# A hybrid attention block: the gate projections as seven half-size products for each pair of column blocks

## The chip, the cores and the metric

The kernel runs on one core of one Trainium2 chip. The metric is the device time of one execution in microseconds (us); three runs of the kernel before gave a median of 1430.39 us (1430.27 to 1430.98). The profile is of one execution.

## What is computed

One encoder block on 1024 tokens of width 1024, with 16 meta tokens put in front and dropped again at the end, all in float32:

```python
h = concat([meta, x])
n = rms_norm(h, norm_mix)
qa, ka, va, qb, kb, vb, ga, gb = split(n @ w_in)     # 512, 512, 512, 512, 128, 128, 1024, 1024 columns
y_a = differential_attention(qa, ka, va, ...)        # branch A: 4 heads, all keys, two softmaxes subtracted
y_b = windowed_gqa(qb, kb, vb, sink)                 # branch B: 8 heads, window of 128, sinks
m = sigmoid(ga) * (y_a @ w_ba) + sigmoid(gb) * (y_b @ w_bb)
h = h + m @ w_o
h = h + swiglu(rms_norm(h, norm_ffn), w_gate, w_up, w_down)
out = rms_norm(h, norm_final)[16:]
```

The change concerns `ga` and `gb`: 2048 columns of `n @ w_in`, for the 1024 real tokens.

## The kernel before, in words

**Products.** The kernel keeps float32 accuracy with three matmuls of rounded operands. An operand is split (`split`, L114 to L117) into a high part, a copy that ScalarE (ACT) rounds, and a low part, the difference, made by GpSimd (POOL) or VectorE (DVE); a product is high x high + high x low + low x high. A group of matmuls gathers in one PSUM bank of 128 x 512 and is then evicted.

**The normalized input** stands in SBUF from the start of branch B to the end of branch A, transposed, as `hT_hi` and `hT_lo` (L173, L174): 128 partitions x 8 chunks of the width x 1088 tokens, the real ones at 0 to 1023, the meta tokens behind.

**Stages and their order.** (1) Norm and transposes of `x`, with the `kb` and `qb` projections between them, up to about 40 us. Behind them stands work on tables of distances (L558 to L600: an integer ramp from POOL; then on DVE conversion, negation and maximum for two halves, `far`, `tbx`, `lam_p`, `nsink`), and DVE's low half of the last `kb` eviction (L251). The `vb` projection follows (`project_v`, L604). (2) Branch B, from about 63 us to 293: units of `attend_b` between the other projections (`project_qa`, `project_kva`, `units_b`, L608 to L664). Queries, keys and values of branch A go to DRAM (`qa_d`, `ka_d`, `va_d`), B's results to `yb_d`. (3) Branch A with the gates, 293 to 622 us. (4) The merge, whose first products are `ppa` (`branch_mm`, L676): eight splits of `yb` (L929 to L939), four sigmoids at a time on loaded gates (`gated`, L987), a DVE multiplication (L1003). Then the output projection and the feed-forward part, which the change leaves alone.

**Weights.** `order` (L200 to L206) lists the column blocks of 128 in the order of use, and `ensure(n)` (L209) loads and splits them until n are ready. A block is 1024 x 128, loaded in one transfer of 512 KB into one of two raw buffers (`preload`, L186); ACT makes the high part whole, 128 x 1024, and POOL the low part (L116).

**Gates before.** `gate_steps` (L682) is a generator of 256 steps of three matmuls of 512 columns: 16 blocks x 2 halves of the tokens x 8 chunks. At the end of each half ACT copies the bank to `gate_stage` and SP stores it to `g_d`, from which the merge reads it.

**What sets the order in branch A.** PE's order is written out by hand (`tc.manual_schedule`, L827). A unit is one head and one tile of 128 queries; 32 units and one more run through a string of slots: `s` scores, `g` one gate step (`fill(1)`), `t` transposes, `n` the value products of earlier units. `SLOTS` (L41) has five `g`, `SLOTS_LAST` (L42), used for the last of the four heads, four. Ahead of head 0 stand `G_FIRST` = 30 gate steps, ahead of each other head `G_HEAD` = 10; `HOLD` = 36 steps are kept back for after the units (L805, L868 to L874). At the start of a head `load_a` (L705) issues the loads of its queries, keys and values. In a unit DVE finds the row minima out of PSUM (L741), combines the two softmaxes (L752, two SBUF operands of 128 x 1040), and makes the low part of the transposed weights (L768, out of PSUM); POOL scales one softmax (L749). The other engines' queues are ordered by the build's scheduler; SP's queue issues nearly all transfers in its order.

Of the kernel before, what the change touches and what calls it, by code (L numbers as in the profile page):

```python
# [9 lines left out]
F32 = mybir.dt.float32  # L10
F32R = mybir.dt.float32r
# [3 lines left out]
ALU = mybir.AluOpType  # L15
# [4 lines left out]
P = 128  # L20
# [53 lines left out]
def encoder_block(ctx: ExitStack, tc: tile.TileContext, x, meta, norm_mix, w_in, lq1, lk1, lq2, lk2,  # L74
# [7 lines left out]
    def f32(ap):  # L82
        return ap.bitcast(F32)
# [13 lines left out]
    def bank(p, tag, name, bufs):  # L97
        return p.tile([P, 512], F32, tag=tag, name=name, bufs=bufs)
# [2 lines left out]
    ka_d = [dram.tile([2, P, L], F32, name=f"ka_d{h}") for h in range(AH)]  # L101
    va_d = [dram.tile([P, 2, 9, P], F32, name=f"va_d{h}") for h in range(AH)]
    g_d = [dram.tile([P, S], F32, name=f"g_d{i}") for i in range(16)]
    ya_d = [dram.tile([P, S], F32, name=f"ya_d{h}") for h in range(4)]
    yb_d = [dram.tile([P, S], F32, name=f"yb_d{h}") for h in range(4)]

# [7 lines left out]
    def split(hi, lo, src, lo_eng):  # L114
        high = nc.scalar.activation(hi, src, AF.Copy)  # L115
        lo_eng.tensor_tensor(lo, src, f32(hi), ALU.subtract)  # L116
        return high  # L117
# [83 lines left out]
    for h in range(AH):  # L201
# [77 lines left out]
    def flush_v():  # L279
        for g in turning_v:  # L280
            for _ in g:
                pass
# [31 lines left out]
    def vb_evac(pt, k0, nb, kp):  # L314
        for g in range(BG):
            src = pt[:, :, 64 * g:64 * g + 64]
            hi = vb[g][:kp, k0:k0 + nb, 0:64]
            lo = vb[g][:kp, k0:k0 + nb, 64:128]
            nc.scalar.activation(hi, src, AF.Copy)
            nc.vector.tensor_tensor(lo, src, f32(hi), ALU.subtract)  # L320

    def new_qb(g):
        return bpool.tile([P, 4, S], F32R, tag="qb", name=f"qb{g}", bufs=1)
# [337 lines left out]
    for h in (2, 3):  # L661
        all_of(project_qa(h))
        project_kva(h)
    flush_v()  # L664
    close_bpool()
    close_psum1()

# [11 lines left out]
                nc.tensor.matmul(ps, w[:, a, j, :], src(j, b, tk),  # L679
                                 start=(j == 0 and n == 0), stop=(j == 3 and n == 2))  # L680

    def gate_steps():  # L682
        for i in range(16):
            def g_evac(ps, at, n, i=i):
                st = gstage.tile([P, 512], F32, tag="g", name="gate_stage", bufs=G_BUFS)
                nc.scalar.copy(st, ps)
                nc.sync.dma_start(g_d[i][:, at:at + n], st)

            ensure(1)
            col = (C_GB if i < 8 else C_GA) + (i % 8) * P  # L690
            for _ in project_steps(col, Q_CHUNKS, f"g{i}", g_evac):
                yield
            ensure(W_BUFS - 1)
# [5 lines left out]
    psum1 = psum2  # L699

    s0s = [apool.tile([P, 9 * P], F32, name=f"as0_{i}") for i in range(2)]
    for i in range(2):
# [897 lines left out]
```

## Time and profile before

| | |
|---|---|
| median of three runs | 1430.39 us |
| span of the profiled execution | 1427.5 us |
| outside the span, by these two | 2.9 us |
| matmul and transpose records of PE | 7279 |
| stage 1, norm and first projections | 0 to 63 us |
| branch B | 63 to 293.4 us |
| branch A with the gates | 293.4 to 621.6 us |
| gate matmuls | 768 of 512 columns |

The profile is of one execution: engines' busy time and its share of the span, the chain of work that ended last followed back from the end, groups of instructions by line, and DMA issues with the median time to landing. PE is the tensor engine's matmuls, PEld its weight loads, which overlap them, SP the queue that issues transfers. In a group's row, "x" is the count, then busy time in us and the mean of one in ns, then the idle time of the engine ahead of them and what ended it. In a timeline row the first two numbers are start and duration in us, and brackets hold the idle time ahead and its releaser. Line numbers are those of the kernel before.

### The profile page before, as it was taken

The page shows a single profiled execution, that of the slowest core. Times are in us where ns is not written, and L with a number is a line of the kernel's source. Part 1 is how long each engine was busy: PE and PEld are TensorE (multiplying, and loading weights), DVE is VectorE, ACT ScalarE, POOL GpSimd, SP SyncE. Part 2 cuts the span into 40 slices and gives each one's busy share as a digit, 9 for nine tenths or more (in the row PEclk, how much of TensorE's full clock was granted, in tenths as well). Part 3 has the DMA queues.
Part 4 walks back from the last instruction along what each step waited for, and adds up shares of the span by engine and source line. Part 5 has one row for each costly group of instructions (what it writes and reads, how often), then busy time and mean ns, then how long its engine had stood idle before and what let it go on. Part 6 is the DMA issues. An engine that isn't in the chain of part 4 may idle for free.

```text
span 1427.5 us, 20915 instructions
## 1 busy us (share of the span) xinstructions
PE 1418.5 (99%) x7279; PEld 1222.2 (86%) x7279; DVE 907.8 (64%) x1808; ACT 673.0 (47%) x1276; POOL 463.7 (32%) x462
## 2 busy tenths in 40 slices
PE   9999999999999999999999999999999999999998
PEld 8998999989898999888888888888888888888886
DVE  6555565528686868446978966555544553787566
ACT  6354555425454546455346654333333333444454
POOL 4143233322232222212503044454444442000442
PEclk9999999999999999999999999999999999999999
DMA  8443443381524252087432724423332232954443
GB/s 240 95 124 104 99 115 106 84 257 48 149 75 157 68 156 68 34 307 242 143 123 82 207 83 145 152 99 104 110 104 96 97 108 99 357 188 141 125 126 148
DMA packets 159018, 191.55 MB, mean 134 GB/s; under 512 B 16104, under 2 KB 103600, under 8 KB 158912
## 3 DMA queue, kind: packets, MB, share of 16 engines
q1 hardware_dynamic: 156992, 187.38, 41.4%
q10 hardware_dynamic: 1920, 2.83, 0.6%
q8 instruction: 58, 0.95, 0.3%
q14 instruction: 48, 0.39, 0.1%
HBM read 129.67 MB, written 53.94 MB: 129 GB/s over the span
## 4 chain that ended last, share of the span: by engine, by line
PE 96%; DMA 1%; DVE 1%; issue 0%; ACT 0%; POOL 0%; SPq 0%; DVEq 0%
PE pg L1363 29%; PE pd L1467 15%; PE pp_g L227 12%; PE ppa L679 5%; PE aps L735 4%; PE po L1266 4%; PE apy L777 3%; PE pp_ka L227 3%; PE pp_va L227 3%; PE pp_qb L227 3%; PE pp_qa L227 3%; PE apt L764 2%; PE bps L358 2%; PE po L1274 2%; PE bpy L398 1%; PE bpt L393 1%
## 5 line engine op out<-in xcount | busy, mean ns | idle before, releaser
L1363 PE MATMUL pg<-t,wop 128*128 128x512 f32 x1056 | 242.4, 389 | 0.0
L1363 PEld LDWEIGHTS pg<-t,wop 128*128 128x128 f32 x1056 | 198.3, 188 | 41.1
L1467 PE MATMUL pd<-ob,oa 128*128 128x512 f32 x924 | 209.6, 389 | 0.0
L1467 PEld LDWEIGHTS pd<-ob,oa 128*128 128x128 f32 x924 | 173.5, 188 | 36.0
L116 POOL TENSOR_TENSOR wop<-wf,wop 128x512 fp32r<-128x512 f32 x114 | 150.5, 1320 | 164.7 <-ACT wop L115 154.7
L1363 PE MATMUL pg<-b,wop 128*128 128x512 f32 x792 | 183.3, 389 | 0.0
L1363 PEld LDWEIGHTS pg<-b,wop 128*128 128x128 f32 x792 | 148.5, 188 | 30.7
L116 POOL TENSOR_TENSOR wl_c<-w_c,wh_c 128x1024 fp32r<-128x1024 f32 x32 | 77.4, 2419 | 137.4 <-ACT wh_c L115 115.7
L115 ACT ACTIVATE wop<-wf 128x512 fp32r<-128x512 f32 x128 | 80.8, 632 | 71.7 <-PE pg L1363 50.5
L746 ACT ACTIVATE as<-as,amn 128x1040 f32<-128x1040 f32 x64 | 74.5, 1165 | 73.8 <-DVE amn L741 73.7
L227 PE MATMUL pp_g<-hT_hi,wh_c 128*128 128x512 f32 x256 | 100.9, 394 | 0.0
L227 PE MATMUL pp_g<-hT_lo,wh_c 128*128 128x512 f32 x256 | 100.4, 392 | 0.0
L227 PE MATMUL pp_g<-hT_hi,wl_c 128*128 128x512 f32 x256 | 100.3, 392 | 0.0
L115 ACT ACTIVATE oa<-ra 128x512 fp32r<-128x512 f32 x77 | 48.7, 632 | 108.5 <-PE pd L1467 50.4
L735 PE MATMUL aps<-ak,aq 128*128 128x352 f32 (+1 forms) x384 | 93.0, 327 | 0.3 <-DMA ak<-ka_d 0.3
L116 POOL TENSOR_TENSOR oa<-ra,oa 128x512 fp32r<-128x512 f32 x27 | 34.9, 1294 | 168.6 <-ACT oa L115 167.2
L1140 DVE TENSOR_TENSOR s<-wf,wf 128x512 f32<-128x512 f32 x22 | 18.2, 827 | 110.4 <-DMA wf<-in_w_ff_up_dram 70.2
L735 PEld LDWEIGHTS aps<-ak,aq 128*128 128x128 f32 x384 | 69.7, 188 | 14.4 <-DMA ak<-ka_d 0.7
L741 DVE CUSTOM_DVE_ANT_0 as<-aps,dist,amn 128x352 f32<-128x352 f32 (+1 forms) x128 | 71.3, 564 | 10.4 <-PE aps L735 8.4
L360 DVE CUSTOM_DVE_ANT_0 bs<-bps,tbx,nsink 128x432 f32<-128x432 f32 (+1 forms) x64 | 38.3, 627 | 53.4 <-PE bps L358 28.9
L370 POOL TENSOR_SCALAR bs<-bs,bdn 128x432 f32<-128x432 f32 (+1 forms) x64 | 36.9, 596 | 97.2 <-DVE bdn L368 69.4
L741 DVE CUSTOM_DVE_ANT_0 as<-aps,dist,far_a 128x352 f32<-128x352 f32 x64 | 37.1, 580 | 42.2 <-PE aps L735 42.1
(290 smaller groups left out, 3029.9 us busy)
## 6 DMA issues: line engine op xcount, KB each, us to landing
ra<-aop SPq DMA_DIRECT2D x77, 256.0 KB, 2.7
w_c<-in_w_in_dram SPq DMA_DIRECT2D x33, 512.0 KB, 4.2
wf<-in_w_ff_gate_dram SPq DMA_DIRECT2D x25, 512.0 KB, 3.6
wf<-in_w_ff_up_dram SPq DMA_DIRECT2D x25, 512.0 KB, 3.6
aop<-as SPq DMA_DIRECT2D x44, 256.0 KB, 2.1
aop<-c SPq DMA_DIRECT2D x33, 256.0 KB, 2.0
g_d<-gate_stage SPq DMA_DIRECT2D x32, 256.0 KB, 2.0
gt<-g_d SPq DMA_DIRECT2D x32, 256.0 KB, 3.6
```

The lines of the kernel that those rows point to most:

```text
L115: high = nc.scalar.activation(hi, src, AF.Copy)
L116: lo_eng.tensor_tensor(lo, src, f32(hi), ALU.subtract)
L227: product = nc.tensor.matmul(ps[:, :n], a[:, c, :], b[:, c, at:at + n], start=(u == 0), stop=(u == 3 * DC - 1))
L360: nc.vector.tensor_tensor_reduce(st[:, r, :W], ps[:, :W], tb, 2.0 ** -(4 * g + r + 1), nsink[:, 4 * g + r:4 * g + r + 1], ALU.add, ALU.min ...
L679: nc.tensor.matmul(ps, w[:, a, j, :], src(j, b, tk), start=(j == 0 and n == 0), stop=(j == 3 and n == 2))
L735: nc.tensor.matmul(ps[:, :n], qs[m][:, t * P:(t + 1) * P], ks[m][:, vv, k0:k0 + n], start=(vv == 0), stop=(vv == 1))
L741: nc.vector.tensor_tensor_reduce(s[m][:, a:b], ps[:, a - k0:b - k0], far_by, slope, low, ALU.add, ALU.min, mn[:, m, i + j:i + j + 1])
L746: nc.scalar.activation(s[m][:, 0:L], s[m][:, 0:L], AF.Exp, bias=low, scale=-1.0, accum_out=dn[:, m:m + 1])
L777: nc.tensor.matmul(py[:, cols], v[:kp, a, k, :], at_[:kp, k, b, :], start=(k == 0 and j == 0), stop=(k == 8))
L1266: nc.tensor.matmul(sets_o[p][u], oa[:, a, u * P:(u + 1) * P], ob[:, b, :], start=(p in (1, 5) and j == 0 and k == 0), stop=(p in (2, 3) an ...
L1363: nc.tensor.matmul(ps, op[:, x, c, :], b[:, y, c, :], start=(p in (1, 5) and c == 0 and n == 0), stop=(p in (4, 2, 3) and c == 3 and n == ...
L1467: nc.tensor.matmul(ps[u], oa[:, a, u * P:(u + 1) * P], ob[:, b, :], start=(p in (1, 2, 5) and j == 0 and k == 0), stop=(p in (2, 3, 4) and ...
```

## The change

Two column blocks of a gate, 2k and 2k+1, and the two halves of the contraction and of the tokens make a 2 x 2 by 2 x 2 block product. It is computed with seven block products instead of eight (Winograd's form of Strassen's method). Each of the 56 products (8 pairs k, seven p) is 12 matmuls of 512 columns: 4 chunks x 3; four steps of three matmuls.

**Order.** In the first pass the pairs' products 1, 2 and 6, in the second 5, 7, 3 and 4 (`order_g`). The first pass reads the four quarters of `hT` as they are, except that product 6 needs a token sum in the quarter (0, 1); the second pass reads token sums in three quarters.

**Token sums.** `tokens_mixed`, a generator advanced once in each `units_b` round and then run out, makes four sums for each of four chunk pairs on POOL: two additions of 128 x 1024 from `hT_hi` and `hT_lo`, four subtractions of 512, then a split (ACT high, POOL low) and a store to the DRAM tiles `t_d`, 16 stores of 512 KB. `turn_into(i)` reads one sum back over a quarter of `hT_hi` and `hT_lo`, 1 MB each: sum 2 at the start of branch A behind `load_a(0)` in the code, sums 0, 1 and 3 after the last three products of the first pass.

**Weights.** Raw blocks are loaded as before but 36 times instead of 16, because the second pass and the middle products need them again; they alternate between two buffers of `wpool` and two new ones of `gstage` (`w2`). POOL makes weight sums (48 of 512) and all low parts (56 of 512), ACT the high parts (56 of 512).

**Evictions.** Products 1 and 2 share a bank. ACT copies out 1 and, after 2, the finished quarter; DVE adds products 6, 5, 7, 3 and 4 to a kept tile (40 additions, PSUM and one SBUF operand). Eight partial sums go to DRAM (`u_d`, 256 KB each) between the passes and come back, one for each pair.

**Slots.** `SLOTS` becomes equal to `SLOTS_LAST`: four gate steps in every unit. `G_FIRST`, `G_HEAD` and `HOLD` stay.

The diff, cut to its core:

```diff
-SLOTS = "sgsgsngsgsgstntnt"
+SLOTS = "sgsgsngsgsstntnt"
...
-    order += [C_GB + i * P for i in range(8)] + [C_GA + i * P for i in range(8)]
...
+    def tokens_mixed():
+        for c in range(4):
+            x = bpool.tile([P, 4, 512], F32, tag="tmix", name=f"tmix_{c}", bufs=1)
+            x11, x12, x21, x22 = (x[:, i] for i in range(4))
+            def whole(i):
+                at = slice(2 * i, 2 * i + 2)
+                src = [f32(h)[:, 4 * i + c, 0:S].rearrange("p (a n) -> p a n", a=2) for h in (hT_hi, hT_lo)]
+                nc.gpsimd.tensor_tensor(x[:, at], src[0], src[1], ALU.add)
+            def kept(k, t):
+                st = bpool.tile([P, 2, 512], F32R, tag=("wh", "wl")[k % 2], name=f"tst{k}_{c}", bufs=1)
+                split(st[:, 0], st[:, 1], t, nc.gpsimd)
+                nc.sync.dma_start(t_d[k][:, :, c, :], f32(st))
+            whole(0)
+            nc.gpsimd.tensor_tensor(x11, x12, x11, ALU.subtract)
+            kept(0, x11)
+            yield
+            whole(1)
+            nc.gpsimd.tensor_tensor(x12, x22, x12, ALU.subtract)
+            kept(1, x12)
+            yield
...
@@ units_b
             pending.append(attend_b(g, t, qb))
+            next(mixing, None)
...
+    first_g = [(k, p) for i in (0, 2) for p in (1, 2) for k in (i, i + 1)] + [(k, 6) for k in range(4)]
+    first_g += [(k, p) for k in range(4, 8) for p in (1, 6, 2)]
+    order_g = first_g + [(k, p) for k in range(8) for p in (5, 7, 3, 4)]
...
+    def load_g():
+        while n_loaded[0] < min(len(loads_g), n_freed[0] + 4):
+            kind, k, i = key = loads_g[n_loaded[0]]
+            p, tag = ((wpool, "w"), (gstage, "w2"))[n_loaded[0] % 2]
+            n_loaded[0] += 1
+            col = G_COLS[k] + i * P
+            w = raw_g[key] = p.tile([P, DC, P], F32, tag=tag, name=f"wg_{kind}{k}_{i}", bufs=2)
+            nc.sync.dma_start(w, w_in[:, col:col + P].rearrange("(c p) n -> p c n", p=P))
...
+    RIGHT_G = {1: (0, 0), 6: (0, 1), 2: (1, 0), 5: (0, 0), 7: (0, 1), 3: (1, 1), 4: (1, 0)}
+    INTO_T = {2: (0, 1), 0: (0, 0), 1: (0, 1), 3: (1, 0)}
+    def turn_into(i):
+        d, t = INTO_T[i]
+        for hl, h in enumerate((hT_hi, hT_lo)):
+            nc.sync.dma_start(f32(h)[:, 4 * d:4 * d + 4, HALF[t]], t_d[i][:, hl])
...
+            for c in range(4):
+                for i, (x, h) in enumerate(((0, hT_hi), (0, hT_lo), (1, hT_hi))):
+                    nc.tensor.matmul(ps, op[:, x, c, :], h[:, 4 * d + c, HALF[t]], ...)
+                if c == 3:
+                    if p == 1:
+                        kept[k] = kept_g(f"p1_{k}")
+                        nc.scalar.copy(kept[k], ps)
...
+                    elif p == 7:
+                        st = stage_g(f"g22_{k}")
+                        add(st, ps, kept.pop("q"), ALU.add)
+                        store(st, 2 * k + 1, 1)
...
+                    if n + 1 == n_first - 2:
+                        turn_into(0)
+                    elif n + 1 == n_first - 1:
+                        turn_into(1)
+                    elif n + 1 == n_first:
+                        turn_into(3)
...
+                yield
+            ensure_g(n + 4)
...
-    n_gates = [256 - HOLD]
+    n_gates = [4 * len(order_g) - HOLD]
...
-                    ensure(2)
-
-                    preload(order[0])
+                    ensure_g(2)
                 ld = load_a(h)
+                if not h:
+                    turn_into(2)
                 fill(G_HEAD if h else G_FIRST)
```

More of the change, by code (lines that the diff above doesn't have):

```diff
@@ L103, in encoder_block @@
     g_d = [dram.tile([P, S], F32, name=f"g_d{i}") for i in range(16)]
+    t_d = [dram.tile([P, 2, 4, 512], F32, name=f"t_d{i}") for i in range(4)]
+    u_d = [dram.tile([P, 512], F32, name=f"u_d{i}") for i in range(8)]
     ya_d = [dram.tile([P, S], F32, name=f"ya_d{h}") for h in range(4)]
@@ L664, in encoder_block @@
     flush_v()
+    for _ in mixing:
+        pass
     close_bpool()
@@ L680, in branch_mm @@
                                  start=(j == 0 and n == 0), stop=(j == 3 and n == 2))
[L682 to L693, printed above, removed]
     close_stage()
@@ L698, in encoder_block @@
     psum2, close_psum2 = pool("psum2", space=PSUM)
-    psum1 = psum2
+    G_COLS = [C_GB + 2 * k * P for k in range(4)] + [C_GA + 2 * k * P for k in range(4)]
+    first_g = [(k, p) for i in (0, 2) for p in (1, 2) for k in (i, i + 1)] + [(k, 6) for k in range(4)]
+    first_g += [(k, p) for k in range(4, 8) for p in (1, 6, 2)]
+    order_g = first_g + [(k, p) for k in range(8) for p in (5, 7, 3, 4)]
+    n_first = len(first_g)
+    uses_g = []
+    for n, (k, p) in enumerate(order_g):
+        if n >= n_first:
+            uses_g.append([("s", k, 1), ("s", k, 0)] if p == 5 else [])
+        elif k < 4:
+            uses_g.append({1: [("f", k, 0)], 2: [], 6: [("m", k, 0), ("m", k, 1)]}[p])
+        else:
+            uses_g.append({1: [("f", k, 0)], 2: [], 6: [("f", k, 1)]}[p])
@@ new lines, in encoder_block, with weights_g @@
+    sums_g = {}
+    def weights_g(n):
+        k, p = order_g[n]
+        load_g()
+        tt = nc.gpsimd.tensor_tensor
+        nm = f"{k}_{p}"
+        kind = "s" if n >= n_first else "f" if k >= 4 or p != 6 else "m"
+        wa, wb = raw_g[kind, k, 0], raw_g.get((kind, k, 1))
+        a11, a12 = wa[:, 0:4], wa[:, 4:8]
+        if wb is not None:
+            a21, a22 = wb[:, 0:4], wb[:, 4:8]
+        done = []
+        if p == 1:
+            src = a11
+        elif p == 2:
+            src, done = a12, ["f"]
+            if k < 4:
+                n_freed[0] += 1
+            else:
+                n_freed[0] += 2
+        elif p == 6:
+            tt(a21, a21, a22, ALU.add)
+            tt(a21, a21, a11, ALU.subtract)
+            src = a21
+            if k < 4:
+                n_freed[0] += 2
+        elif p == 5:
+            src = sums_g[k] = gstage.tile([P, 4, P], F32, tag="s", name=f"s1g_{k}", bufs=1)
+            tt(src, a21, a22, ALU.add)
+        elif p == 7:
+            tt(a21, a11, a21, ALU.subtract)
+            src = a21
+        elif p == 3:
+            tt(a12, a12, a11, ALU.add)
+            tt(a12, a12, sums_g.pop(k), ALU.subtract)
+            src = a12
+        else:
+            src = a22
+            n_freed[0] += 2
+        op = ops_g[n] = wpool.tile([P, 2, 4, P], F32R, tag=("wh", "wl")[n % 2], name=f"wopg_{nm}", bufs=W_BUFS)
+        split(op[:, 0], op[:, 1], src, nc.gpsimd)
```

60 lines of the change are left out of this document (added).

## The prediction

> **What bounds the kernel now.** I read the page's busy shares first, then the chain by engine, then the groups of the lines that the diff touches.
>
> ```profile
> span 1427.5 us, 20915 instructions
> ...
> PE 1418.5 (99%) x7279; PEld 1222.2 (86%) x7279; DVE 907.8 (64%) x1808; ACT 673.0 (47%) x1276; POOL 463.7 (32%) x462
> ...
> PE 96%; DMA 1%; DVE 1%; issue 0%; ACT 0%; POOL 0%; SPq 0%; DVEq 0%
> ...
> L116 POOL TENSOR_TENSOR wop<-wf,wop 128x512 fp32r<-128x512 f32 x114 | 150.5, 1320 | 164.7 <-ACT wop L115 154.7
> ...
> L116 POOL TENSOR_TENSOR wl_c<-w_c,wh_c 128x1024 fp32r<-128x1024 f32 x32 | 77.4, 2419 | 137.4 <-ACT wh_c L115 115.7
> L115 ACT ACTIVATE wop<-wf 128x512 fp32r<-128x512 f32 x128 | 80.8, 632 | 71.7 <-PE pg L1363 50.5
> ...
> L227 PE MATMUL pp_g<-hT_hi,wh_c 128*128 128x512 f32 x256 | 100.9, 394 | 0.0
> ...
> w_c<-in_w_in_dram SPq DMA_DIRECT2D x33, 512.0 KB, 4.2
> ```
>
> PE is the kernel: 99% busy, 96% of the chain. Every matmul removed is time saved, and every wait that PE is given is time lost in full, since there is nearly no idle time to absorb it. The last column of the pp_g row (idle before, 0.0) says the same of the gates.
>
> The chain in order of time (start, us, what) gives the true price of a matmul, since the 394 ns of a group overlap one another:
>
> ```profile
> 51.47 10.21 PE pp_vb L227 x63
> ...
> 293.38 20.45 PE pp_g L227 x90
> ...
> 621.55 2.27 PE ppa L679 x10
> ```
>
> 20.45 us for 90 matmuls is **0.227 us** for one of 512 columns. The windows (us, then busy time and count of PE, PEld, DVE, ACT, POOL, then clock, DMA share, GB/s) show how full PE is by stage:
>
> ```profile
> 63.00:293.40 230.40, 230.40 (x1333) 210.08 (x1332) 131.77 (x346) 120.80 (x289) 75.35 (x97) 1.00 0.40 110
> 293.40:316.00 22.60, 22.60 (x102) 18.78 (x102) 1.63 (x5) 4.38 (x7) 4.79 (x2) 1.00 1.02 304
> 545.12:575.16 30.04, 30.04 (x196) 27.71 (x196) 26.50 (x91) 17.67 (x34) 9.06 (x11) 1.00 0.14 45
> ```
>
> PE is full in branch B (to 293.4), at the start of branch A and in its units. The third row holds four units of head 3, which already have the slots (four gate steps) that the change gives to all: 7.51 us a unit, with DVE at 6.62. Median 1430.39 less span 1427.5 leaves 2.9 us outside the span, which I keep.
>
> **The change part by part.**
>
> *Removed matmuls.* 16 projections x 2 halves x 24 = 768 become 56 products x 12 = 672. 96 x 0.227 = **-21.8 us**, at full clock (1.00 in the rows).
>
> *Token sums at the head of B.* The built queues put ten reading POOL operations right behind the norm: two adds of 1024, four subtractions and two low halves of 512, and the weight splits of VB and QA0. In before POOL is idle there and DVE clears its own work:
>
> ```profile
> 39.47 0.65 DVE L562 CAST dist<-it 128x960 f32<-128x960 int32 x1
> 40.16 0.66 DVE L564 TENSOR_SCALAR neg<-dist 128x960 f32<-128x960 f32 x1
> ...
> 41.13 1.15 DVE L565 TENSOR_TENSOR dist<-dist,neg 128x960 f32<-128x960 f32 x1
> ...
> 46.40 0.55 DVE L569 TENSOR_TENSOR tbx<-dist,far 128x384 f32<-128x384 f32 x1
> ...
> 46.93 2.31 DVE L589 TENSOR_SCALAR nsink<-sinkb 128x8 f32<-128x8 f32 x1
> ...
> 49.87 0.44 DVE L251 TENSOR_TENSOR qk_stage<-pp_kb,qk_stage 128x272 fp32r<-128x272 f32 x1 [0.52 <-ACT qk_stage L250]
> ```
>
> ```profile
> 46.76 2.45 POOL L116 TENSOR_TENSOR wl_c<-w_c,wh_c 128x1024 fp32r<-128x1024 f32 x1 [10.87 <-ACT lam_s L599]
> 49.63 2.40 POOL L116 TENSOR_TENSOR wl_c<-w_c,wh_c 128x1024 fp32r<-128x1024 f32 x1 [0.42 <-ACT wh_c L115]
> ```
>
> nsink, eight columns, takes 2.31 us: it ends as POOL's operation of 46.76 ends. The L251 eviction reads PSUM and one SBUF operand and takes 0.44 beside POOL's operation of 49.63. So SBUF-only DVE work and POOL tensor work take turns; PSUM evictions don't. Later, where both have work:
>
> ```profile
> 676.09 0.68 DVE L116 TENSOR_TENSOR oa_o<-m,oa_o 128x512 fp32r<-128x512 f32 x1
> ...
> 678.63 1.55 DVE L116 TENSOR_TENSOR oa_o<-m,oa_o 128x512 fp32r<-128x512 f32 x1 [0.15 <-ACT oa_o L115]
> ```
>
> ```profile
> 676.25 3.38 POOL L1034 TENSOR_TENSOR m<-gt,m 128x512 f32<-128x512 f32 x2 [1.23 <-DVE gt L1029]
> ```
>
> The first low half runs ahead of POOL's two additions in 0.68, the second beside them in 1.55. I take strict alternation. Ten such DVE operations (L562 to L589 and lam_p, 6.7 us by these rows: the two rounds of 0.65 + 0.66 + 1.15, and under 2 for the rest) stand ahead of the last kb eviction. POOL's ten, by the L116 rows, are 4 x 2.42 + 6 x 1.32 = 17.6 us. From hT's last low half (39.2 us) that is 39.2 + 17.6 + 6.7 = 63.5, less about 1 at the ends: the eviction comes at 62.5, not 49.9. The first pp_vb matmul takes that PSUM bank (so the built program waits) and runs at 51.47 now: PE, with everything queued behind that matmul, stands still for **+11 us**. If POOL lets several DVE operations through in a row, it is 5; 13 if one more of its operations comes first.
>
> [...]
>
> *Token sums later in B.* VA0's low weights stand behind the next two adds of 1024; stepping POOL's queue by the L116 prices makes them ready about 1.6 us after PE, 11 us late itself, wants them: +1.6 (0 to 3). The rest has slack: the sums are 4 rounds of 2 x 2.42 + 8 x 1.32 = 15.4 us, some 50 us of them after the head, and POOL is busy for 75 of the 230 us (window of 63.00). ACT's 16 high halves of 0.63 and 16 stores of 512 KB lie under 121 us of ACT work and a DMA share of 0.40: 0. DVE's short SBUF operations in each unit wait their turn now and then: +1.5 (0 to 4).
>
> *Start of A.* SP's queue has the reload of the first quarter (2 x 1 MB, once the last ka matmul has read it, about 292) ahead of the raw weights of the second product, and these wait for its landing; the last ka_d and yb_d stores and head 0's loads are queued behind it as well. At the 304 GB/s of the window, 2.1 MB take 6.9 us: landed by 300. The weights take 4.2, then 0.63 (ACT) and 1.32 (POOL): 306.5. PE wants them after the first product, 293.4 + 12 x 0.227 = 296.1. **+10.5 us** (6 if the loads overlap, 14 if other loads share the rate). The third pair's product may wait for its own weights, +1 (0 to 4). The loads of head 0 come later too, but the stall and 30 gate steps of 0.68 us cover them. The other three quarters are reloaded two units or more ahead of use (15 us against 7), and behind them SP has only gate stores and weights that are two products early: 0.
>
> *Units of A.* Evictions move from ACT to DVE in the second pass and POOL sums run beside.
>
> ```profile
> L752 DVE SCALAR_TENSOR_TENSOR as<-as,adn,as 128x1040 f32<-128x1040 f32 x32 | 41.5, 1297 | 1.5
> L686 ACT COPY gate_stage<-pp_g 128x512 f32<-128x512 f32 x32 | 18.4, 576 | 35.7 <-PE pp_g L227 14.1 <-issue 12.4 <-DMA ka_d<-qk_stage 7.9
> L1003 DVE TENSOR_TENSOR m<-gt,ppa 128x512 f32<-128x512 f32 x16 | 10.8, 684 | 12.0 <-ACT gt L991 9.6 <-PE ppa L679 2.2 <-issue 0.2
> ```
>
> A gate addition has the operands of L1003, 0.68. A unit's four steps are one product, so DVE has 6.62 + 0.68 = 7.30 a unit, and with a share of a 1.30 us L752 that waits its turn against POOL's sums (some 0.25) 7.55 to PE's 7.51: level, with no room for waits. I take 0.2 us in each of the second pass's 18 units: **+4** (0 to 12). POOL itself has 56 splits and 48 sums of 512, 104 x 1.32 = 137 us in 328: no bound.
>
> *End of the gates.*
>
> ```profile
> 619.89 3.77 ACT L115 ACTIVATE yb<-m 128x512 fp32r<-128x512 f32 x6 [0.51 <-issue]
> ...
> 624.15 1.28 ACT L991 ACT_TABLE_LOAD   x1
> 625.44 2.19 ACT L991 ACTIVATE gt<-gt 128x512 f32<-128x512 f32 x4
> ```
>
> ```profile
> 618.41 5.98 DVE L116 TENSOR_TENSOR yb<-m,yb 128x512 fp32r<-128x512 f32 x8 [9.04 <-ACT yb L115]
> ```
>
> In before the yb splits run under the last gate steps, and the first ppa follows at 621.55 without a gap. After the change ACT's queue has the table load, the four sigmoids (1.28 + 2.19) and a weight split ahead of them, and DVE's eight low halves stand behind the last gate addition: the first ppa group needs six of the eight, 1.28 + 2.19 + 0.63 + 6 x 0.63 = 7.9 us after the gates' end, and ends near 8.2 where 12 x 0.227 = 2.7 would do: **+5.5** (0 to 8).
>
> Sum: -21.8 + 11 + 1.6 + 1.5 + 10.5 + 1 + 4 + 5.5 = **+13.3**. Span 1440.8, with 2.9 outside it **1443.7 us**. All low ends: 1430.4 - 10.8 = 1419.6; all high ends: 1430.4 + 36.2 = 1466.6.
>
> **Rivals.**
> 1. *The other side: the SBUF operations of DVE and POOL don't take turns, or hardly do.* Place: B's head first, then the units. Price: the 11 us, the 1.5 of B's units and the 4 of A's (where 7.30 stays below 7.51): 1443.7 - 16.5 = **1427.2**, 0.2% faster. It decides from a kb eviction before 54, a stall of under 3. For it: L562 and L565 show their short times here, if only because POOL idles. Against: nsink, and L116 at 678.63.
> 2. *The transfers and the splits are in time:* the reload overlaps the weights (stall 6) and the yb splits hide under the gates' last steps: 1443.7 - 4.5 - 5.5 = **1433.7**. For it: the 304 GB/s were shared with head 0's loads, which now come behind. Against: the weights wait for the reload to land, not only to be issued. With rival 1 it gives **1417.2**.
> 3. *DVE is the bound of the second pass:* units of 7.9 to 8.0 instead of 7.51, since L752, L116 and the additions lose more turns: +8 more, **1452**. For it: 6.62 of 7.51 are used already. Against: evictions from PSUM don't take turns.
>
> That the products don't shrink is excluded: the built program has 672 gate matmuls.
>
> **How the numbers follow.** Forecast (within 8 us) 0.47, rival 1 alone 0.18, rivals 1 and 2 together 0.09, rival 2 alone 0.08, rival 3 0.18. A measurement can tell about 0.2% from no change here, 2.9 us. Of rival 1 alone 0.10 is faster than that, 0.05 within and 0.03 slower; of rival 2 alone 0.02 within, 0.06 slower. Faster 0.10 + 0.09 = 0.19, same 0.07, slower 0.47 + 0.18 + 0.03 + 0.06 = 0.74. The range 1421 to 1460 takes in every case but the two together (1417, of whose 0.09 a third may reach 1421) and the far end of rival 3: some 0.06 lie below and 0.08 above.
>
> **What would show it.** Right: a PE gap of about 11 us ahead of pp_vb with L598 to L625 of the new numbering stretched by POOL; a second gap of about 10 ahead of the second gate product; 672 gate matmuls at 0.227; second-pass units of 7.6 to 7.9; a gap of 4 to 6 around the first ppa. Wrong: nsink done by 50, the second product at 296, or units beyond 7.9.

## The result, and the profile after

The changed kernel takes **1487.76 us** (median of four, 1485.59 to 1490.88), the kernel before beside it 1430.33: a ratio of 1.0404 (95% interval 1.0388 to 1.0420), 57.4 us slower. Forecast was 1443.7, range 1421 to 1460: the sign was right, the size a quarter of what came. The profiled execution took 1490.88 us, 1489.1 of it in the span, 61.6 more than the span before; 1.8 us lie outside it (the 2.9 in the table of the kernel before paired a median with the span of one execution). One execution of e10 below took 5013 us against 1450 to 1455 for the other three, and e10's median leaves it out.

The page of the changed kernel, the lines that answer to those of before; the new one is PEclk, the granted clock in tenths over 40 slices:

```profile
span 1489.1 us, 21073 instructions
...
PE 1425.3 (96%) x7183; PEld 1221.6 (82%) x7183; DVE 951.8 (64%) x1848; ACT 688.7 (46%) x1316; POOL 634.8 (43%) x590
...
PEclk9999999988999999998999999999999999999999
...
PE 82%; DMA 6%; DVE 5%; POOL 3%; issue 2%; ACT 1%; SPq 1%; ACTq 0%; DVEq 0%; POOLq 0%
```

PE has 96 instructions fewer, as planned, but is busy 6.8 us *more*, and idle for 63.8 us where it was idle for 9. Its share of the chain fell from 96% to 82%. The waits of PE by what ended them (us in total, times, longest) name the places:

```profile
PE apt L940 <- DVE as L928: 12.7, 6, 3.6
PE ppa L718 <- ACT yb L117: 9.0, 1, 9.0
PE pg L837 <- ACT wopg L117: 8.6, 1, 8.6
PE pp_vb L228 <- DVE qk_stage L252: 6.6, 1, 6.6
PE aps L911 <- DVE at L944: 5.0, 5, 3.7
PE pg L837 <- POOL wopg L118: 3.0, 1, 3.0
```

Branch A as one window, from the first gate matmul to the first ppa, before and then after (columns as in the prediction: length, busy time and count of PE, PEld, DVE, ACT, POOL, clock, DMA share, GB/s):

```profile
293.40:621.60 328.20, 327.86 (x1937) 293.77 (x1937) 220.65 (x725) 161.21 (x294) 93.09 (x92) 1.00 0.37 115
```

```profile
319.70:324.50 4.80, 4.62 (x10) 3.23 (x11) 0.00 (x0) 0.51 (x1) 2.50 (x2) 0.52 1.04 317
...
308.20:678.90 370.70, 327.14 (x1841) 288.67 (x1841) 248.52 (x761) 172.59 (x320) 196.00 (x183) 0.93 0.54 171
```

PE's work there should be 327.9 - 21.8 = 306.1 us. It takes 370.7: 43.6 us idle, and 327.1 - 306.1 = 21.0 us in which PE is busy longer with the same work. The row of 319.70 shows such a stretch, behind the pause ahead of the second product: clock 0.52 and 10 matmuls in 4.8 us. An estimate of what the clock took: PE's busy time in windows of half a us, times what the granted clock lacks of 1.00 there, sums to some 17 us over A, so the clock carries most of the 21.0; what the other 4 are stays open. The whole ledger: -21.8 (matmuls), +43.3 more idle time in A and +21.0 more busy time there, +6.8 up to pp_vb (58.25 for 51.47), +8.0 from there to A (308.18 for 293.38), +4.2 behind the first ppa; in all +61.5.

### The profile page after: what moved, and what is told of

It reads as the page before. It is cut to its first block, busy times and chain, and to the rows that moved or that the text cites. A ratio compares the mean times of both kernels' runs of the same rounds, so it can differ in the third digit from the quotient of the medians.

```text
span 1489.1 us, 21073 instructions
## 1 busy us (share of the span) xinstructions
PE 1425.3 (96%) x7183; PEld 1221.6 (82%) x7183; DVE 951.8 (64%) x1848; ACT 688.7 (46%) x1316; POOL 634.8 (43%) x590
## 4 chain that ended last, share of the span: by engine, by line
PE 82%; DMA 6%; DVE 5%; POOL 3%; issue 2%; ACT 1%; SPq 1%; ACTq 0%; DVEq 0%; POOLq 0%
PE pg L1539 28%; PE pd L1643 14%; PE pg L837 5%; PE ppa L718 5%; PE po L1442 4%; PE pp_ka L228 3%; PE pp_qb L228 3%; PE pp_va L228 3%; PE pp_qa L228 3%; PE apy L953 2%; PE aps L911 2%; DMA wg_s<-in_w_in_dram 2%; PE bps L394 2%; PE po L1450 1%; DVE as L917 1%
## 5 line engine op out<-in xcount | busy, mean ns | idle before, releaser
L837 PE MATMUL pg<-hT_hi,wopg 128*128 128x512 f32 x448 | 166.4, 403 | 13.4 <-ACT wopg L117 8.6
L837 PEld LDWEIGHTS pg<-hT_hi,wopg 128*128 128x128 f32 x448 | 86.4, 193 | 28.8 <-ACT wopg L117 9.0
L837 PE MATMUL pg<-hT_lo,wopg 128*128 128x512 f32 x224 | 89.6, 400 | 0.0
L1316 DVE TENSOR_TENSOR s<-wf,wf 128x512 f32<-128x512 f32 x22 | 16.8, 762 | 113.1 <-DMA wf<-in_w_ff_up_dram 70.1
L917 DVE CUSTOM_DVE_ANT_0 as<-aps,dist,amn 128x320 f32<-128x320 f32 (+1 forms) x128 | 71.1, 561 | 7.3 <-PE aps L911 5.4
L406 POOL TENSOR_SCALAR bs<-bs,bdn 128x432 f32<-128x432 f32 (+1 forms) x64 | 36.9, 596 | 71.8 <-DVE bdn L404 40.7
L917 DVE CUSTOM_DVE_ANT_0 as<-aps,dist,far_a 128x352 f32<-128x352 f32 x64 | 36.9, 577 | 45.5 <-POOL wg_m L776 32.5
L940 PE MATMUL apt<-ident,as 128*128 128x128 f32 x288 | 49.9, 296 | 15.7 <-DVE as L928 12.7
```

The costliest lines, as they stand in the source:

```text
L837: nc.tensor.matmul(ps, op[:, x, c, :], h[:, 4 * d + c, HALF[t]], start=(p in (1, 6, 5, 7) and c == 0 and i == 0), stop=(p in (2, 6, 3, 4) ...
L917: nc.vector.tensor_tensor_reduce(s[m][:, a:b], ps[:, a - k0:b - k0], far_by, slope, low, ALU.add, ALU.min, mn[:, m, i + j:i + j + 1])
L940: nc.tensor.transpose(pt[:kp, j, :], s[:, k * P:k * P + kp], ident)
```

## The experiments

Medians in us, each beside the kernel before on its own chip (1430.3 to 1431.5). "A" is the stage from the first gate matmul to the first ppa in the profiled execution, with PE's idle time, and its busy time over 306.1, from the window of that stage. The executions of the changed kernel spread over 5.3 us and the profiled one is its slowest, so a few us of difference in A say nothing.

| kernel | median | A | idle | over |
|---|---|---|---|---|
| changed | 1487.8 | 370.7 | 43.6 | 21.0 |
| e1 sums late | 1473.0 | 365.6 | 42.7 | 16.8 |
| e2 reload late | 1479.4 | 360.5 | 38.3 | 16.1 |
| e3 scaling on ACT | 1486.0 | 364.0 | 40.7 | 17.1 |
| e4 merge order | 1480.1 | 356.8 | 33.4 | 17.3 |
| e5 no reloading of weights | 1467.2 | 346.6 | 29.0 | 11.5 |
| e8 mended | 1467.4 | 358.3 | 32.5 | 19.7 |
| e9 spread first pass | 1442.9 | 333.5 | 18.2 | 9.2 |
| e10 spread, scaling on ACT | 1453.9 | 343.1 | 23.0 | 14.0 |
| e11, e12 other order | 1449.9, 1450.3 | 336.9, 340.7 | 19.1, 20.1 | 11.7, 14.5 |
| e13 as e9, no reloading | 1427.5 | 317.5 | 7.4 | 4.0 |
| e14 as e9, no weight sums | 1427.7 | 319.6 | 7.5 | 6.0 |
| e15 as e9, neither | 1422.5 | 312.3 | 3.9 | 2.3 |

### One mend at a time (e1 to e4)

**e1**, the sums held behind the second unit's last POOL operation:

```diff
-            next(mixing, None)
+            with tc.issue_after(unit_ends[1].ins):
+                next(mixing, None)
```

> The changed kernel with one edit: the token sums are queued on POOL behind the second unit of branch B instead of right behind the norm. Theory of the turns (SBUF operations of DVE and POOL exclude each other): the pause of 6.6 us ahead of pp_vb and the slow matmuls behind it (11.9 us for 63 where before has 10.2) go, 8 us less than the changed kernel's 1487.8, so about 1480. Rival (POOL's late weight split of VB holds PE, not DVE): the split is early in this kernel as well, so the time would be the same, and only DVE's rows tell: nsink and the distance operations short (0.65, 1.15) by the theory, still stretched by the rival. If nothing but the order of work on POOL counts later on, the sums may push the weight splits of branch B back by up to 3 us.

In the changed kernel the rows of DVE and of POOL at the head of B show the turns:

```profile
49.53 3.23 DVE L601 TENSOR_TENSOR dist<-dist,neg 128x960 f32<-128x960 f32 x1
...
54.13 2.58 DVE L605 TENSOR_TENSOR tbx<-dist,far 128x384 f32<-128x384 f32 x1
...
57.77 0.43 DVE L252 TENSOR_TENSOR qk_stage<-pp_kb,qk_stage 128x272 fp32r<-128x272 f32 x1
```

```profile
48.93 2.81 POOL L118 TENSOR_TENSOR wl_c<-w_c,wh_c 128x1024 fp32r<-128x1024 f32 x1
51.70 2.18 POOL L349 TENSOR_TENSOR tmix<-tmix 128x512 f32<-128x512 f32 x1
```

DVE's maximum of 49.53 ends at 52.76, about its own 1.15 behind the end of POOL's operation of 48.93 (51.74); POOL's of 51.70 takes 2.18 for 1.3 with DVE's in front. In e1 the maximum is short again and pp_vb starts at 51.5 without a wait; one turn is left, tbx behind the weight split of VB (46.95, 2.40), as nsink had it in before:

```profile
44.51 1.16 DVE L605 TENSOR_TENSOR dist<-dist,neg 128x960 f32<-128x960 f32 x1
...
47.10 2.67 DVE L609 TENSOR_TENSOR tbx<-dist,far 128x384 f32<-128x384 f32 x1
...
50.07 0.44 DVE L252 TENSOR_TENSOR qk_stage<-pp_kb,qk_stage 128x272 fp32r<-128x272 f32 x1
```

1473.0, 14.8 less: more than the 8 expected. A starts at 295.5 instead of 308.2, so by the profiled executions the early sums had cost the rest of branch B another 4 us beside the 8.5 at its head, and A itself was 5 shorter.

**e2**, the reload behind head 0's loads:

```diff
-                    turn_into(2)
+                    with tc.issue_after(loaded_a[0].ins):
+                        turn_into(2)
```

> The changed kernel with one edit: the first reload of the normalized input stands in SP's queue behind the loads of head 0 instead of ahead of the second product's weights. Theory (the weights wait for the reload's landing): the pause of 8.6 us ahead of the second gate product and the half-speed matmuls behind it go, 10 to 11 us less than 1487.8. Rival (the transfers of this stretch are bound by bandwidth, 313 to 353 GB/s at a DMA share over 1): the same bytes have to land, so the pause only moves to head 0's queries or to the first product that needs the reload: less than 4 us gained.

1479.4, 8.4 less, but the pause ahead of the second product only fell from 8.6 to 6.2: its weights' load is now issued at 315.12, right behind B's last yb_d stores in SP's queue (311.90 to 314.4). The reload was the first of two things in the way. The rest of A's 10.2 us is in the units and in PE's excess, which fell from 21.0 to 16.1; two further waits for weights, 2.7 us each (345.62 and 349.07), stand where the changed kernel has one of 3.0. The gain lies between the theory's 10 to 11 us and the rival's 4.

**e3**, the softmax scaling off POOL:

```diff
-                (nc.gpsimd if t % 4 in COMBINE_POOL else nc.vector).tensor_scalar(
-                    s[1][:, 0:L], s[1][:, 0:L], dn[:, 1:2], neglam, ALU.mult, ALU.mult)
+                nc.vector.tensor_tensor(dn[:, 1:2], dn[:, 1:2], neglam, ALU.mult)
+                nc.scalar.activation(s[1][:, 0:L], s[1][:, 0:L], AF.Copy, scale=dn[:, 1:2])
```

> The changed kernel with one edit: the scaling of one softmax (128 x 1040) goes from POOL to ACT, and the small copy behind the combination from POOL to DVE. Theory (POOL's queue: a weight sum that waits for its transfer stands ahead of this scaling, DVE's combination and PE's transposes wait for it): the 13 us that PE waits for the combination shrink to under 4 and the slow matmuls behind those pauses go, 20 to 30 us less than 1487.8. Rival 1 (DVE is the bound in the units): DVE has a little more work here, so the time stays or grows by up to 5 us. Rival 2 (the raw weights are late for the products themselves): the pauses move from the transposes to the gate products, under 10 us gained.

1486.0, 1.7 less, which is within the spread of the executions: the theory as stated fell. The small copy behind the combination goes from POOL to DVE here as well. PE's wait for DVE's combination is 12.2 us, as it was 12.7. ACT's own queue shows why, in e3:

```profile
350.69 0.63 ACT L117 ACTIVATE wopg<-wg_m 128x512 fp32r<-128x512 f32 x1 [3.72 <-POOL wg_m L776]
351.23 1.15 ACT L926 ACTIVATE as<-as,adn 128x1040 f32<-128x1040 f32 x1
352.29 1.15 ACT L922 ACTIVATE as<-as,amn 128x1040 f32<-128x1040 f32 x1
```

The high half of a weight waits 3.72 us for POOL's sum, with the scaling and the exponential queued behind it. Softmax work stands behind weight work on either engine, so moving it from one to the other gained nothing here.

**e4**, ACT's order at the merge:

```diff
-        gate_ops.append(nc.scalar.activation(gt, gt, AF.Sigmoid))
+        with tc.issue_after(yb_last.ins):
+            gate_ops.append(nc.scalar.activation(gt, gt, AF.Sigmoid))
```

> The changed kernel with one edit: on ACT the splits of branch B's result stand ahead of the first sigmoids and the third branch weight. Theory (the sigmoids wait for their gate loads and hold up the splits): the pause of 9.0 us at the first ppa shrinks to 2 to 3 and the slow matmuls behind it go, 8 to 10 us less than 1487.8. Rival (the splits wait for memory that the last gate addition and its store release, whatever the order): 3 us or less gained.

1480.1, 7.7 less, about what was expected; PE's waits ahead of ppa are 1.2 us at most instead of 9.0. In the changed kernel ACT's rows show the order:

```profile
665.96 1.28 ACT L1167 ACT_TABLE_LOAD   x1
673.48 0.63 ACT L1167 ACTIVATE gt<-gt 128x512 f32<-128x512 f32 x1 [6.24 <-DMA gt<-g_d]
...
677.68 0.63 ACT L117 ACTIVATE wbhb<-wbrb 128x512 fp32r<-128x512 f32 x1
678.21 2.17 ACT L117 ACTIVATE yb<-m 128x512 fp32r<-128x512 f32 x4
```

The first sigmoid waits 6.24 us for its gate, and the splits wait behind it.

### What a pause costs (e6, e7)

Both start from the kernel before; the long one has `range(3)`, the short one `range(0)`:

```diff
+    def held(st, wh):
+        scr = wpool.tile([P, 512], F32, tag="scr", ...)
+        for _ in range(3):
+            nc.gpsimd.tensor_tensor(scr, st, st, ALU.add)
+            st = scr
+        nc.gpsimd.tensor_scalar(scr[:, 0:P], st[:, 0:P], 0.0, 0.0, ALU.mult, ALU.mult)
+        w = wpool.tile([P, DC, P], F32R, tag="held", ...)
+        nc.gpsimd.tensor_tensor(w[:, 0, :], f32(wh)[:, 0, :], scr[:, 0:P], ALU.add)
+        return w
```

> The kernel before with three forced pauses of PE ahead of head 0: at three of the gates' half blocks the first weights are made anew by POOL from the evicted half before (a 128 x 128 scaling by 0 and an addition), so that PE stands for about 1.6 to 2 us each time. Theory (the granted clock halves only after a pause of several us): the time grows by the pauses alone, 5 to 6 us. Rival (any pause costs clock): 10 us or more.

> The same with three additions of 128 x 512 more in POOL's chain: about 6 us for each of three pauses, 18 us in all. Theory (after a pause of several us the clock is granted at half for some us more): the time grows by the pauses and 1.5 to 3 us behind each, 22 to 27 us. Rival (a pause costs only itself, and the slow matmuls of the changed kernel have another cause, such as contention): 18 us, all matmuls at 0.227.

1457.5 and 1470.6, 27.2 and 40.3 us over the kernel before. The pauses were longer than planned. The short kernel's first matmuls behind them, and the 3 to 4 us that follow:

```profile
304.92 0.80 PE L242 MATMUL pp_g<-hT_hi,held 128*128 128x512 f32 x1 [5.81 <-POOL held L226]
...
317.36 0.80 PE L242 MATMUL pp_g<-hT_hi,held 128*128 128x512 f32 x1 [4.19 <-POOL held L226]
...
326.25 0.50 PE L242 MATMUL pp_g<-hT_hi,held 128*128 128x512 f32 x1 [1.67 <-POOL held L226]
```

```profile
304.90:308.90 4.00, 3.98 (x9) 3.14 (x10) 0.00 (x0) 0.00 (x0) 0.00 (x0) 0.50 1.06 251
317.40:320.40 3.00, 3.00 (x7) 2.43 (x8) 0.00 (x0) 0.00 (x0) 0.00 (x0) 0.50 0.62 180
326.30:330.30 4.00, 4.00 (x18) 3.31 (x19) 0.00 (x0) 0.00 (x0) 0.00 (x0) 1.00 0.11 41
```

Behind 5.81 and 4.19 us the clock is granted at 0.50 and 4 us hold 9 matmuls instead of 18; behind 1.67 us it stays at 1.00. The 90 matmuls ahead of head 0 took 37.0 us here (293.46 to 330.46): 20.46 as before, 11.67 of pauses and 4.9 more. The long kernel, behind its second and third pause:

```profile
324.00:328.00 4.00, 4.00 (x10) 3.13 (x11) 0.00 (x0) 0.00 (x0) 0.00 (x0) 0.50 0.02 4
337.50:341.50 4.00, 4.00 (x10) 3.13 (x11) 0.00 (x0) 0.00 (x0) 0.00 (x0) 0.50 0.00 0
```

There the pauses are 8.96, 7.54 and 5.01, all followed by half speed; 50.2 us (294.29 to 344.51) are 20.46 + 21.5 + 8.3. So each of these five pauses of 4 us or more cost itself and 2 to 3 us beside, and contention is no part of it: these two windows have a DMA share of 0.02 and 0.00, and DVE, ACT and POOL do nothing in them. e7's rival falls with that; e6's theory holds for its third pause alone, as the other two came out longer.

The two kernels have no pause between 1.67 and 4.19 us; the changed kernel has, and half speed follows shorter pauses there too:

```profile
487.29 0.66 PE L940 MATMUL apt<-ident,as 128*128 128x128 f32 x4 [2.31 <-DVE as L928]
...
560.06 1.12 PE L940 MATMUL apt<-ident,as 128*128 128x128 f32 x4 [2.52 <-DVE as L928]
```

```profile
442.00:450.00 8.00, 8.00 (x31) 7.46 (x32) 5.08 (x24) 3.53 (x7) 5.91 (x6) 0.50 0.26 85
488.50:490.50 2.00, 2.00 (x11) 2.00 (x11) 2.00 (x7) 0.74 (x2) 2.00 (x3) 0.50 1.05 247
560.10:562.10 2.00, 2.00 (x10) 2.00 (x11) 1.32 (x8) 0.83 (x2) 1.38 (x2) 0.50 1.10 327
```

In the changed kernel the four pauses of 3.68 us or more (3.68, 6.57, 8.57 and 9.01) were followed by 0.50, as were the five above of e6 and e7. Below that some slowed PE and some did not: at the start of A the matmuls behind one of 1.62 us slowed from 0.23 us each to 0.43 in e15 (297.31) and did not in e13 (296.69), and behind one of 2.89 us in e12 (599.35) the next five of the gates still came 0.23 us apart. So the traces give no sharp limit. The half speed can also last: behind the pause of 3.68 us (441.82) PE was busy for 8 us on end at 0.50. By the estimate above that stretch alone took over 4 us, the two short pauses 1.6 and 1.7.

What neither expectation foresaw, in PE's waits of the short and of the long kernel:

```profile
PE ppa L694 <- ACT yb L115: 7.6, 1, 7.6
```

```profile
PE ppa L694 <- ACT yb L115: 8.0, 1, 8.0
```

Both pause ahead of ppa, with gates otherwise as before. They hold 6 KB a partition more in a pool on the right side. In the built programs the last yb tile then shares memory with a gate tile that is still to be stored, which it doesn't in the kernel before, and ACT's order puts the sigmoids first. So the merge's pause came without the seven products, in two kernels that only hold more of SBUF and pause earlier; that the shared memory is what moves ACT's order was not tested by itself.

### What holds the units (e5, e13, e14, e15)

**e5** loads four raw blocks and uses them throughout:

```diff
+            if n_loaded[0] > 4:
+                raw_g[key] = four[(n_loaded[0] - 1) % 4]
+                continue
```

> The changed kernel with one edit: of the 36 raw weight blocks only the first four are loaded, the others reuse those four tiles, so that the weight sums and splits of later products never wait for a transfer (the gates' values are then not the reference's; matmuls, splits, sums and evictions are as many). Theory (in the units the in-order queues of POOL and ACT stand at weight work whose raw block has not landed, and the softmax work queued behind it is late): the pauses between 347 and 632 us, 22 us in all, shrink to under 8, and most of the half-speed clock behind them goes: 25 to 35 us less than 1487.8. Rival 1 (the sums and splits themselves occupy POOL and take turns with DVE's combination): all of that work remains, under 8 us gained. Rival 2 (DVE's 40 additions): they remain as well, under 8 us gained.

1467.2, 20.6 less, under the 25 to 35 expected; A is 24.1 shorter. The splits, sums and additions are all there, so transfers are on the path, if not alone: PE's pauses in the units (of 0.3 us and more, 347 to 632 us) fall from 21.3 us to 8.6. The chain of the changed kernel, in order of time ahead of the longest pause of a unit (aps waits 3.68 us at 441.82):

```profile
415.05 9.45 DMA wg_s<-in_w_in_dram
...
430.56 1.24 POOL wopg L118
...
431.82 4.31 DMA wg_s<-in_w_in_dram
...
436.26 1.28 POOL wg_s L787
437.55 1.20 POOL as L925
...
438.81 2.18 issue
441.00 0.69 DVE at L944
```

POOL's low half at 430.56 releases a raw buffer; only then is the next load issued, 4.31 us; POOL's queue stands at the sum that needs it (436.26) for 4.32 us; the scaling L925 comes behind the sum, DVE's combination behind that (438.78 to 441, 2.30 us for some 1.30, with a low half of POOL's beside it at 438.71), and PE behind all. Each engine has room on the average: of the 370.7 us of A, DVE is busy for 248.5, POOL for 196.0 and ACT for 172.6. In series the links take 10 us from the load's issue to PE, and PE stands still for 3.68 of them.

One pause is of another kind. It is the same 3.6 us in the changed kernel and in e5:

```profile
636.48 1.09 PE L940 MATMUL apt<-ident,as 128*128 128x128 f32 x4 [3.61 <-DVE as L928]
```

With `HOLD` left at 36, 224 - 36 = 188 gate steps stand ahead of the end of the units, and 30 + 3 x 10 + 32 x 4 uses them all: the one turn behind the 32 units has none to cover its softmax, where the kernel before had 8 left. HOLD 32, with other edits in e9, leaves 0.8 us of it.

e13 to e15 repeat this on the best mended kernel, e9 below: e13 leaves out the reloading, e14 POOL's weight sums, e15 both, so that like e5 they don't compute the gates.

> The kernel with the spread first pass (1442.9 us), with only the first four of 36 raw weight blocks loaded and reused (the gates' values are then not the reference's). If transfers carry the rest: 10 us or more less, at or below the kernel before's 1430. If POOL's sums and turns carry it: under 4 us less.

> The same kernel with all 36 transfers but none of the 48 weight sums (the gates' values are then not the reference's); splits and additions stay. If POOL's sums carry the rest: 10 us or more less. If transfers carry it: under 4 us less.

> The same kernel with neither (values not the reference's). What stays above 1412 us then is neither: the reload, the additions on DVE, the merge and the start of A. Expected 1420 to 1428.

1427.5, 1427.7 and 1422.5. Taking away *either* recovers 14 to 15 us of e9's time, both 19 to 20 (e9 ran on another chip): not additive, which fits the chain, for a sum that need not wait, or a wait that blocks no sum, does no harm. POOL is as busy in e13 as in e9, and DVE too:

```profile
296.30:629.80 333.50, 315.33 (x1840) 278.67 (x1840) 243.34 (x761) 166.20 (x311) 192.02 (x181) 0.98 0.57 179
```

```profile
296.70:614.20 317.50, 310.12 (x1841) 277.20 (x1841) 242.46 (x761) 165.39 (x311) 190.34 (x179) 0.99 0.42 135
```

192.0 against 190.3 and 243.3 against 242.5 us. So neither POOL's amount of work nor DVE's additions bound branch A: e13 has them all at 7.4 us of idle time.

### Mended kernels (e8 to e12)

**e8** joins e1, e4 and HOLD 32 with another first pass:

```diff
+    first_g = [(k, p) for p in (1, 2, 6) for k in (0, 1)]
+    first_g += [(k, p) for k in range(2, 8) for p in (1, 6, 2)]
...
+            with tc.issue_after(load_ins[-1].ins) if load_ins else ExitStack():
...
+                    with tc.issue_after(load_ins[3].ins):
+                        turn_into(2)
```

> The changed kernel with the mends together: sums behind the second unit of branch B, splits of branch B's result ahead of the sigmoids, HOLD 32 so that the last unit has gate steps, and a first pass whose pairs 0 and 1 take products 1, 2 and then 6 from one pair of raw blocks and the other pairs 1, 6, 2 (32 raw loads for 36), with the first four raw loads ahead of the reload and this ahead of head 0's loads. If the named waits carry the loss: 14.8 + 8.4 + 7.7 of the three single edits, 5 for the last unit and its clock, 10 or more for the burst of raw loads: 1435 to 1442. If the 21.8 us of removed matmuls come free entirely: 1412. Rival (POOL's and DVE's own work bounds the units): 1452 or more.

1467.4, a miss by 25 us. Of the 32.5 us of idle time in A 14.0 are now waits for weights at its start; SP's queue and the window of PE's longest pause:

```profile
316.68 10.22 SPq L757 DMA_DIRECT2D wg_f<-in_w_in_dram  x4
```

```profile
320.00:330.00 10.00, 2.39 (x6) 1.42 (x6) 0.69 (x1) 1.15 (x2) 2.44 (x2) 0.61 1.03 309
```

The weights of the seventh product stand behind the reload and head 0's loads, the DMA share is over 1, and PE is busy 2.4 of 10 us. So bytes look like the bound here; e9 goes on from that.

**e9** keeps the changed kernel's order of products with e1, e2, e4 and HOLD 32, loads the first two raw blocks during branch B, and starts the units earlier:

```diff
-G_HEAD = 10
-G_FIRST = 30
+G_HEAD = 12
+G_FIRST = 24
...
-            p, tag = ((wpool, "w"), (gstage, "w2"))[n_loaded[0] % 2]
+            p, tag = ((wpool, "w"), (wpool, "w"), (gstage, "w2"), (gstage, "w2"))[n_loaded[0] % 4]
```

> The changed kernel with its own order of products and these mends: sums behind the second unit of branch B; splits of branch B's result ahead of the sigmoids; raw blocks loaded in the order of use, the first two into the buffers that are free in branch B; the reload behind head 0's loads; 24 gate steps ahead of head 0 and 12 ahead of the other heads instead of 30 and 10, HOLD 32, so that the four products that need two raw blocks each fall into units of 7.5 us. The run before this one, with the reload ahead of head 0's loads and a denser burst of raw blocks, stood still for 15 us between 299 and 337 at 309 to 345 GB/s. Theory (at the start of A it is bytes in time that bind): the pauses ahead of the second to the sixth product go, PE stands for under 6 us in 295 to 340: 1440 to 1450. Rival (POOL's and ACT's queues bind at the start whatever the transfers): 1460 to 1468.

1442.9 (ratio 1.0081, 1.0064 to 1.0097), as expected: 45 of the 57 us are back, in A mostly. The edits were not run one by one. That this is near the forecast is chance: several other waits are gone here.

> The same with the softmax scaling on ACT instead of POOL. If scaling behind POOL's weight work still costs pauses ahead of the transposes: 5 to 10 us less than the kernel beside it. If DVE's work bounds the units by then: the same or up to 5 us more.

1453.9, 11 more than e9 and outside both figures; DVE, with the small products and the copy, is busy 266.6 us in A against 243.3, and its combination again ends most of the waits of the transposes. On this kernel POOL is the better place.

**e11** puts pair 4 between the eight single-block products and the four that need two (`first_g[8:8] = [(4, p) for p in (1, 6, 2)]`), with 26 and 10 gate steps and HOLD 36; **e12** also makes weights one product less ahead (`ensure_g(n + 3)`) and moves two raw buffers to another place.

> The kernel of the run with the spread first pass, with two more edits: pair 4 takes its products 1, 6 and 2 between the first eight products and the four that need two raw blocks each (a fifth tile for kept partial sums), and 26 and 10 gate steps ahead of the heads, HOLD 36. There the remaining pauses were 6.5 us at 316 to 334 (head 0's keys, then the weights of the ninth product) with half speed behind them, and 2.6 at the merge. If bytes in time bind the start, the ninth product's weights are there when wanted: 4 to 8 us less than 1442.9, 1435 to 1439. Rival (the reload is then what the ninth and tenth products wait for): the same time.

> The same with weights made one product less ahead, so that fewer weight sums that wait for a raw block stand in POOL's queue ahead of softmax work, and the two raw buffers of the second pool at its lower end. If sums made too early still hold up POOL: 2 to 4 us less than the kernel beside it. If the weights get late instead: 2 to 6 us more.

1449.9 and 1450.3: both miss, 7 more than e9, and e12's edits make no difference together. The waits of the transposes for DVE's combination are back at 6.8 and 7.9 us, from 1.4 in e9; why was not traced. No version of the seven products that computes the gates beat the kernel before.

## Why the prediction was wrong, point by point

- **Removed matmuls, -21.8.** Right: 672 gate matmuls, and at full clock 0.227.
- **Head of B, +11.** DVE and POOL do take turns (DVE's maximum of 1.15 us took 3.23 at 49.53, with POOL's operations beside it), though what makes them no run shows, and the size was near: a pause of 6.6 us, and 63 pp_vb matmuls that took 11.93 us for 10.21; 8.5 in all. The turns didn't alternate strictly, and POOL's last two low halves came after nsink, so the eviction ran at 57.8 and not at 62.5. e1 shows it: 8.5 us of it go.
- **Later in B, +3.1.** 6.3 by the profile, some 4 of which go in e1; 1.8 is a wait of the first gate product for a late last unit (DVE's `by`), which no step had.
- **Start of A, +10.5.** Near in size: 8.6 us of pause, and some 10 matmuls at half speed, which the step did not have. (Its own addends end at 306.2, not 306.5.) e2 adds that B's last stores stand ahead in the same queue, which the step had put behind the reload and not ahead of the weights.
- **Units of A, +4 (with +1 for the third pair): this step failed.** It counted POOL's work, "137 us in 328: no bound", and DVE's, "level", and called later weights "two products early: 0". The counts hold: the second pass's units mostly run at 7.57 us, and e13 shows POOL's and DVE's amounts harmless. What failed is the step from an engine's amount of work to its waits: it took weights as ready two products early, and an engine with room on the average stood still at the head of its queue. The loop from raw buffer to load to sum to split to buffer came late, and softmax work was queued behind it on POOL and on ACT. Of the 43.6 us of idle time in A, 21 are pauses inside the units, 8.6 stand ahead of the second product, 9.0 ahead of ppa, and 3.6 in the last turn, for which no gate steps were left and which no step of the sum had. e5 takes 13 of the 21 away without reloading.
- **A term was missing: the clock.** Every stall was priced at its own length, "at full clock (1.00 in the rows)", but those rows were of a kernel without pauses. PE was busy 21.0 us longer in A, some 17 of them at a lower clock by the estimate above, and about 2 behind pp_vb's pause. e6 and e7 show it as an effect of pauses.
- **End of the gates, +5.5.** Right in the order of the queues, short in size: 9.0 us and a slow start behind, since the sigmoids wait for their loads, which the sum took as landed.
- **The rivals.** Rival 3 (DVE the bound) had the direction but not the cause; e13 excludes it. Rival 1 falls with e1, rival 2 with the pauses of 8.6 and 9.0 us.

What stays open is the 13.7 us between e15 (1422.5) and 1430.6 - 21.8 = 1408.8, the time if the change cost nothing (the 1412 in two expectations was put 3 too high). By its profiled execution about 6 are in A, 3.9 ahead of it and 5.4 behind the first ppa (15 in all, by the spans of two single executions); they weren't taken apart.

## What to carry to other kernels

In a kernel like this one, with PE 99% busy, a change that saves matmuls and adds preparation is judged by its longest chain from buffer to load to preparation, and by what is queued behind each link, not by busy shares. Price a pause of PE of 3.7 us or more with 2 to 4 us beside its length (4.9 us for two in e6, 8.3 for three in e7, over 4 by the estimate behind the one of 3.68), and expect that some shorter ones cost too (1.6 and 1.7 by the estimate behind 2.52 and 2.31 us). Two kernels that hold 6 KB a partition more in a pool waited 7.6 and 8.0 us at ppa, a stage far from it: compare the order of the queues there too. When steps that fill waits become fewer, count those left for the last turn.

## What the runs showed of the hardware

The changed kernel's four PE pauses from 3.68 us (441.82) up and the five of e6 and e7 ahead of head 0 (4.19 to 8.96) were followed by a clock of 0.50, which lasted 9 us behind that of 3.68; behind shorter ones the matmuls ran at half pace in some cases (1.62 us in e15, 2.31 in the changed kernel) and at full pace in others (1.62 in e13, 2.89 in e12). Strict turns of DVE and POOL were an upper bound: the eviction behind ten DVE operations came 7.9 us later than in before, and not 12.6. With the DMA share over 1 the start of A moved 309 GB/s in e8 and 317 in the changed kernel, and where head 1's loads shared the engines a 512 KB block of weights took 9.45 us (415.05, at a share of 0.85) instead of the 4.2 that is the median in before.
